# Fourth gated head: both value and gate groups by block products, score levels added on VectorE

## The chip, the core and the metric

The kernel runs on one core of one Trainium2 chip. The metric is the device time of one execution in microseconds (us): 1372.14 us, the median of three runs (1371.32 to 1372.71). One execution was profiled as well; it took 1371.82 us, and its trace spans 1370.1 us from the first to the last instruction.

Five engines work side by side, each through its own queue in order: TensorE (PE in the profile, with its weight loads as PEld), VectorE (DVE), ScalarE (ACT), GpSimd (POOL) and SyncE (SP). The last two issue most of the transfers here. SBUF is the memory that the engines compute from, PSUM holds the sums of the matrix products in banks of 128x512 float32.

## The reference

Two layers over 256 tokens of width 2048: a gated linear attention layer (GLA, 4 heads, chunked), then a retention layer (8 heads). Cut to what matters here, a GLA head computes

```
q, k, v, gate = split(rms_norm(x) @ w_in)
log_a  = log_sigmoid((h @ w_a1) @ w_a2 + b_a) / 16
scores = einsum('bhtk,bhsk,bhtsk->bhts', q * 256**-0.5, k, decay)   # causal, decay from cumsum(log_a)
o      = einsum('bhts,bhsv->bhtv', scores, v) + state part
o      = o * rsqrt(mean(o * o) + 1e-6) * head_g
x      = x + (o * silu(gate)) @ w_out
```

Everything is float32. A head's `v` and `gate` are 1024 columns wide each, which the kernel treats as two groups of 512 columns: head 3 has the groups 6 and 7.

## The kernel before, in words

**Precision.** Each float32 operand of a large product is held as two parts, `hi` and `lo`, of a rounded matrix format, and a product is three matrix products: hi by hi, hi by lo, lo by hi. The activations are split once (`xhl`). The weights come from memory in blocks `raw` of 128x1024 (two slices of 128 rows by 512 columns, called a sub here) and each is split when its turn comes: ScalarE writes `hi` (L298), then VectorE writes `lo` as the difference (L299). There are four buffers for `hi` and four for `lo`, and the code splits up to three subs ahead of the one in use (`LOOK = 3`). A sub that multiplies both halves of the tokens takes twelve 512-column products on TensorE, a sub of a block product (below) takes six.

**A plain group.** `group_x` runs the eight subs of a group for both token halves: 96 products. L341 to L343 are its three products; the results are called `gv_ps` (values) and `gg_ps` (gates).

**A joint pair.** `values_and_gates` computes values and gates of one group together. For the first half of the contraction it replaces the eight block products (two token halves, two halves of the rows, values and gates) by seven, in the manner of Strassen and Winograd; `P1`, `P2`, `P3`, `P5`, `P6`, `P7` and `P8` are these products, 12 matrix products each. The second half is done directly (`v4` to `v7`, `g4` to `g7`, 12 each). The order is the string `UNIT`: `P1 v4 z P3 v5 P5 v6 P6 P2 v7 P7 g4 g5 P8 g6 g7`. The weights' sums are made in place: six transfers per pair, issued by GpSimd, add a block from memory to one already loaded (L310), and two VectorE additions (L293) add one raw block to another. A pair therefore loads 14 blocks plainly and 6 by adding, and splits 22 subs, where two plain groups load and split 16. Its results are called `ge_ps`, its products are L413 to L415. After `P5`, `P6`, `P7`, `v7` and `g7` pieces are copied or combined on ScalarE (L1389, L1394, L1404) and VectorE (L1434, L1437, L1440, L1443, L1395, L1402).

**Which pairs are joint.** `JOINT["a"] = (5, 7)`: groups 5 and 7 of the GLA layer, that is the second groups of heads 2 and 3. Groups 4 and 6 are plain.

**Scores of a head.** `gla_scores` works through seven levels of block size 1 to 64: per level VectorE forms differences of the cumulated decay (L792, L800), ScalarE an exponential (L801), VectorE two products (L802, L803), and TensorE a 128x128 product (L764, `lv`). Then VectorE masks the seven results into `m` (L821, L823), GpSimd adds them level by level into `s32`, two instructions per level (L830), and the sum is split into `sc` (L724, L725). `o_part` multiplies `sc` by the values of a group (L698 to L700). These pieces are generators: `advance()` is called after each sub or block product, and takes one more step of them. For a joint second group, `joint_turn` calls `o_part(0)` after `v4` and `o_part(1)` after `g5`.

**Order and buffers.** The order on each engine is set by the tile framework's scheduler, which places instructions by a simulated timeline; what is written later can thus be placed earlier on its engine, and a piece can be put between other work. Inside an engine nothing overtakes. PSUM banks 0 to 3 (`slots`) rotate: a plain group takes two and rotates by two, a joint pair takes four and rotates by two, and `slots` is set anew to 2, 3, 0, 1 ahead of the output projection `gb`.

Of the kernel before, what the change touches and what calls it, by code (L numbers as in the profile page):

```python
# [15 lines left out]
ALU = mybir.AluOpType  # L16

P = 128
# [143 lines left out]
def ret_order(h):  # L162
# [4 lines left out]
HEAD = 4  # L167
EARLY = 2
JOINT = {
    "a": (5, 7),  # L170
    ("ao", 0): (True, True),
    ("ao", 1): (False, True),
    ("ro", 0): (False, True),
# [5 lines left out]
def kernel(  # L179
# [18 lines left out]
    nc = tc.nc  # L198
# [117 lines left out]
    def advance(n=1):  # L316
        for _ in range(n):
            while side:
                try:
                    next(side[0])  # L320
                    break
                except StopIteration:
                    side.popleft()
# [429 lines left out]
    def gla_scores(h, box):  # L753
# [5 lines left out]
        s32 = sc_p.tile([P, 3, P], F32, tag="s32", name=f"s32_{h}", bufs=1)  # L759
        tt = nc.vector.tensor_tensor  # L760
# [22 lines left out]
        for li, B in enumerate(LEVELS):  # L783
            n = P // B
# [35 lines left out]
        m = t4_p.tile([P, 8, P], F32, tag="t4", name=f"m{h}")  # L820
# [3 lines left out]
        nc.vector.tensor_scalar(s32[:, 1, :], ps[1][:, 3, :], SCALE, None, ALU.mult)  # L824
        yield
        for li, B in enumerate(LEVELS):
            for z in range(2):
                side_of = lambda a, h: a.rearrange("p (n h i) -> p n h i", h=2, i=B)[:, :, h, :]
                dst = side_of(s32[:, 2 * z, :], 1 - z)
                nc.gpsimd.tensor_tensor(dst, dst, side_of(m[:, li, :], z), ALU.add)  # L830
            if li == 3:
                yield
        yield
# [3 lines left out]
    def gla_head(h):  # L837
# [10 lines left out]
        def scores():  # L848
            yield from gla_scores(h, hw)
# [16 lines left out]
        def o_part(gi):  # L866
            g = 2 * h + gi
            if gi == 0:
                drain_side()
            po = [mis_p.tile([P, GW], F32, tag="mis", name=f"go{g}_ps{t}") for t in range(2)]  # L870
            o_mms(hw["sc"], vs[gi], po)
            o = o_p.tile([P, 2, GW], F32, tag="o", name=f"go{g}")
            with tc.high_priority():
                for t in range(2):
                    nc.scalar.activation(o[:, t, :], po[t], AF.Copy, scale=r[:, t : t + 1])
                    nc.scalar.activation(po[t], o[:, t, :], AF.Square, accum_out=sso[:, t, gi : gi + 1])
            os_.append(o)
            if gi == 1:
                side.append(og_part(0))
# [26 lines left out]
            )  # L906

        def joint_turn(tok):
            if tok == "v4":
                o_part(0)  # L910
            elif tok == "g5":
                o_part(1)
            else:
                advance()
# [674 lines left out]
```

## Time and profile before

| What | Value |
| --- | --- |
| time, median of 3 (range) | 1372.14 us (1371.32 to 1372.71) |
| profiled execution | 1371.82 us, span 1370.1 us |
| busy: PE, DVE, ACT, POOL | 1360.1, 1098.9, 846.7, 137.2 us |
| head 3: q and k; group 6 values; group 6 gates; group 7 | from about 448, 472, 497 and 520 us; `gb` begins at 564.8 us |

A row of the timeline reads: start, duration, engine, line and operation, what it writes and reads; in square brackets the idle time before it and what ended that. A row of the groups reads: line, engine, operation, shapes, count, then busy time and mean duration in ns of one, then idle time. In the table by stretches each engine's busy time has its instruction count behind it in brackets, then come the granted TensorE clock, the share of the DMA engines and GB/s. In such rows the line numbers are those of the kernel before.

### The profile page before, as it was taken

To read this page: it belongs to the slowest core of one execution; us is meant where nothing else is said; L and a number is where in the kernel's file an instruction comes from. 1 tells how busy PE (TensorE), PEld (TensorE's weight loads), DVE (VectorE), ACT (ScalarE), POOL (GpSimd) and SP (SyncE) were. 2 spreads that over 40 slices of the span, in tenths; PEclk is the share of its full clock that TensorE was granted. 3 is DMA by queue.
4 is the path that set the end of the run, shared out by engine and by line. 5 is a ranking of instruction groups with operands and counts; after the bars stand their busy time and mean duration, and the time that the engine had idled before them with its cause. 6 is when DMAs were issued, how large, how long until landed. Compare 5 with 4: busy or idle time off the path is not lost.

```text
span 1370.1 us, 18374 instructions
## 1 busy us (share of the span) xinstructions
PE 1360.1 (99%) x6564; PEld 1142.3 (83%) x6564; DVE 1098.9 (80%) x1520; ACT 846.7 (62%) x1119; POOL 137.2 (10%) x194
## 2 busy tenths in 40 slices
PE   9999999999999999999999999999999999999997
PEld 7888888888888888888888888888888888888886
DVE  6686795987878886769887988897867898889796
ACT  6576656656567756656666566655546666666565
POOL 1003020110021021001011010100101101010010
PEclk9999999999999999999999999999999999999999
DMA  9755565789658667868897878796798797879773
GB/s 363 255 175 168 169 208 184 154 251 316 202 154 259 201 207 180 326 169 232 260 336 199 259 203 249 209 320 212 172 365 219 245 253 208 268 188 322 237 177 124
DMA packets 84508, 315.04 MB, mean 230 GB/s; under 512 B 9776, under 2 KB 10800, under 8 KB 83136
## 3 DMA queue, kind: packets, MB, share of 16 engines
q1 hardware_dynamic: 67200, 241.63, 50.6%
q0 software_dynamic: 15920, 64.89, 23.7%
q10 hardware_dynamic: 1296, 7.35, 1.4%
q8 instruction: 51, 0.84, 0.2%
q14 instruction: 41, 0.34, 0.1%
HBM read 303.35 MB, written 10.49 MB: 229 GB/s over the span
## 4 chain that ended last, share of the span: by engine, by line
PE 99%; DMA 1%; DVE 0%; ACT 0%; issue 0%; DVEq 0%; ACTq 0%
PE rqk_ps L382 9%; PE re_ps L413 8%; PE re_ps L414 8%; PE re_ps L415 8%; PE rqk_ps L384 4%; PE gqk_ps L382 4%; PE gg_ps L342 3%; PE gv_ps L343 3%; PE gv_ps L341 3%; PE gv_ps L342 3%; PE gg_ps L343 3%; PE gg_ps L341 3%; PE gqk_ps L384 2%; PE ge_ps L415 2%; PE ge_ps L414 2%; PE ge_ps L413 2%
## 5 line engine op out<-in xcount | busy, mean ns | idle before, releaser
L299 DVE TENSOR_TENSOR lo<-raw,hi 128x1024 fp32r<-128x1024 f32 (+1 forms) x568 | 687.4, 1220 | 215.1 <-ACT hi L298 205.1
L298 ACT ACTIVATE hi<-raw 128x1024 fp32r<-128x1024 f32 (+1 forms) x568 | 596.3, 1056 | 398.9 <-PE rqk_ps L382 50.4
L382 PE MATMUL rqk_ps<-xhl,hi 128*128 128x512 f32 x512 | 160.0, 395 | 0.0
L415 PE MATMUL re_ps<-hi,xhl 128*128 128x512 f32 x352 | 137.1, 389 | 0.0
L414 PE MATMUL re_ps<-lo,xhl 128*128 128x512 f32 x352 | 137.1, 389 | 0.0
L413 PE MATMUL re_ps<-hi,xhl 128*128 128x512 f32 x352 | 132.3, 391 | 0.0
L310 POOL DMA_DIRECT2D raw<-in_w_all x90 | 78.0, 868 | 540.5 <-DVE lo L299 205.2
L384 PEld LDWEIGHTS rqk_ps<-xhl,lo 128*128 128x128 f32 x512 | 93.6, 188 | 20.3
L384 PE MATMUL rqk_ps<-xhl,lo 128*128 128x256 f32 x512 | 99.2, 279 | 0.0
L382 PEld LDWEIGHTS rqk_ps<-xhl,hi 128*128 128x128 f32 x512 | 80.7, 189 | 2.8
L382 PE MATMUL gqk_ps<-xhl,hi 128*128 128x512 f32 x256 | 79.5, 397 | 0.6 <-DVE xhl L550 0.6
L414 PEld LDWEIGHTS re_ps<-lo,xhl 128*128 128x128 f32 x352 | 66.1, 188 | 13.6
L415 PEld LDWEIGHTS re_ps<-hi,xhl 128*128 128x128 f32 x352 | 66.1, 188 | 13.6
L413 PEld LDWEIGHTS re_ps<-hi,xhl 128*128 128x128 f32 x352 | 65.9, 188 | 13.3
L342 PE MATMUL gg_ps<-lo,xhl 128*128 128x512 f32 x192 | 75.4, 393 | 0.0
L343 PE MATMUL gg_ps<-hi,xhl 128*128 128x512 f32 x192 | 75.1, 391 | 0.0
L342 PE MATMUL gv_ps<-lo,xhl 128*128 128x512 f32 x192 | 75.1, 391 | 0.0
L341 PE MATMUL gv_ps<-hi,xhl 128*128 128x512 f32 x192 | 75.0, 393 | 0.0
L341 PE MATMUL gg_ps<-hi,xhl 128*128 128x512 f32 x192 | 74.9, 391 | 0.0
L343 PE MATMUL gv_ps<-hi,xhl 128*128 128x512 f32 x192 | 74.8, 391 | 0.0
L830 POOL TENSOR_TENSOR s<-s,m 128x64 f32<-128x64 f32 x56 | 36.5, 684 | 232.3 <-DVE m L821 222.5
L384 PEld LDWEIGHTS gqk_ps<-xhl,lo 128*128 128x128 f32 x256 | 46.1, 188 | 10.0
(422 smaller groups left out, 2591.9 us busy)
## 6 DMA issues: line engine op xcount, KB each, us to landing
raw<-in_w_all SPq DMA_DIRECT2D x449, 512.0 KB, 4.9
raw<-in_w_all POOLq DMA_DIRECT2D x90, 512.0 KB, 7.2
resid<-in_x_n SPq DMA_DIRECT2D x2, 1024.0 KB, 9.8
gg<-in_gn_g POOLq DMA_DIRECT2D x8, 256.0 KB, 4.4
resid_x<-resid ACTq DMA_DIRECT2D x1, 2048.0 KB, 8.5
gb<-in_gn_b POOLq DMA_DIRECT2D x8, 256.0 KB, 4.9
gb_resid<-resid_x POOLq DMA_DIRECT2D x1, 2048.0 KB, 11.0
resid_g<-gb_resid ACTq DMA_DIRECT2D x1, 2048.0 KB, 9.0
```

The costliest lines, as they stand in the source:

```text
L298: a = nc.scalar.activation(hi[:, sl], src[:, sl], AF.Copy)
L299: b = nc.vector.tensor_tensor(lo[:, sl], src[:, sl], hi[:, sl].bitcast(F32), ALU.subtract)
L310: nc.gpsimd.dma_start(raws[n], block(key), accum_op=ALU.add)
L341: pin(mm(ps, xh, hi[:, q, :], start=kt == 0, stop=False, **onto))
L342: pin(mm(ps, xh, lo[:, q, :], start=False, stop=False, **onto))
L343: pin(mm(ps, xl, hi[:, q, :], start=False, stop=kt == end - 1, **onto))
L382: x = mm(ps[c], part, rhs[:, kt, :, :], start=kt == 0, stop=kt == NKT - 1)
L384: x = mm(ps[c][:, 0, :], part, rhs[:, kt, 0, :], start=False, stop=False)
L413: pin(mm(ps, xh, hi[:, q, :], start=start, stop=False, **again))
L414: pin(mm(ps, xh, lo[:, q, :], start=False, stop=False, **again))
L415: pin(mm(ps, xl, hi[:, q, :], start=False, stop=stop, **again))
L830: nc.gpsimd.tensor_tensor(dst, dst, side_of(m[:, li, :], z), ALU.add)
```

## The change

Group 6, head 3's first, becomes a joint pair like group 7. Since both groups of that head are joint now, `joint_turn` does nothing special in the first of them, and in the second one `o_part(0)` comes after `v6` for head 3 (head 2 keeps `v4`). In all four heads the seven levels are added to `s32` by VectorE instead of GpSimd, with one instruction per level that takes both halves.

```
-    "a": (5, 7),
+    "a": (5, 6, 7),
...
         for li, B in enumerate(LEVELS):
-            for z in range(2):
-                side_of = lambda a, h: a.rearrange("p (n h i) -> p n h i", h=2, i=B)[:, :, h, :]
-                dst = side_of(s32[:, 2 * z, :], 1 - z)
-                nc.gpsimd.tensor_tensor(dst, dst, side_of(m[:, li, :], z), ALU.add)
+            n = P // (2 * B)
+            dst = at(s32, B, (2 * P - B, 2), (2 * B, n), (1, B))
+            tt(dst, dst, at(m, li * P, (B, 2), (2 * B, n), (1, B)), ALU.add)
             if li == 3:
                 yield
...
         def joint_turn(tok):
-            if tok == "v4":
+            if gi and tok == ("v6" if h == 3 else "v4"):
                 o_part(0)
-            elif tok == "g5":
+            elif gi and tok == "g5":
                 o_part(1)
```

One line fewer stands in the new file, so its line numbers after L829 are smaller by one.

How the scheduler places this is seen in three places. The first is VectorE's queue in group 6, between the `lo` of the ninth sub of the group (number 186 of the kernel, both times) and the next; `w3` are the score pieces of head 3, `raw154` and `raw155` the two blocks that are added to. Before:

```order
L299 TENSOR_TENSOR lo186_4395<-raw162_4207,hi186_4394 128x1024
L802 TENSOR_TENSOR w3_5_4410<-w3_5_4410,qk3_4238 128x2x4x32
L803 TENSOR_TENSOR w3_5_4410<-w3_5_4410,qk3_4238 128x2x4x32
L798 TENSOR_TENSOR w3_6_4436<-ref3_4437,lc3_4028 128x2x64
L799 TENSOR_TENSOR w3_6_4436<-lc3_4028 128x2x64
L800 TENSOR_TENSOR w3_6_4436<-lc3_4028 128x2x2x64
L812 TENSOR_TENSOR w3_x_4466<-tot3_4029,lc3_4028 128x256 x2
L299 TENSOR_TENSOR lo187_4421<-raw163_4251,hi187_4420 128x1024
```

Now:

```order
L299 TENSOR_TENSOR lo186_4334<-raw160_4131,hi186_4333 128x1024
L293 TENSOR_TENSOR raw154_3958<-raw154_3958,raw157_4041 128x1024
L802 TENSOR_TENSOR w3_2_4324<-w3_2_4324,qk3_4219 128x2x32x4
L803 TENSOR_TENSOR w3_2_4324<-w3_2_4324,qk3_4219 128x2x32x4
L293 TENSOR_TENSOR raw155_3985<-raw155_3985,raw158_4069 128x1024
L792 TENSOR_TENSOR w3_4_4384<-lc3_4007 128x2x8x16
L800 TENSOR_TENSOR w3_4_4384<-lc3_4007 128x2x8x16
L802 TENSOR_TENSOR w3_3_4351<-w3_3_4351,qk3_4219 128x2x16x8
L803 TENSOR_TENSOR w3_3_4351<-w3_3_4351,qk3_4219 128x2x16x8
L792 TENSOR_TENSOR w3_5_4410<-lc3_4007 128x2x4x32
L800 TENSOR_TENSOR w3_5_4410<-lc3_4007 128x2x4x32
L299 TENSOR_TENSOR lo187_4360<-raw154_3958,hi187_4359 128x1024
```

The two additions of raw blocks now stand between these two splits, and the same sub number meets score work that is two levels further back.

The second place is TensorE's queue around the second to last direct step of group 6 (`g6`, sub 198), in the kernel as changed; `ge6_ps1` and `ge6_ps0` are the gate sums of the two token halves:

```order
L413 MATMUL ge6_ps0_4233<-hi198_4565,xhl_105 128x512
L414 MATMUL ge6_ps1_4234<-lo198_4566,xhl_105 128x512
L415 MATMUL ge6_ps1_4234<-hi198_4565,xhl_105 128x512
L413 MATMUL ge6_ps1_4234<-hi198_4565,xhl_105 128x512
L414 MATMUL ge6_ps1_4234<-lo198_4566,xhl_105 128x512
L415 MATMUL ge6_ps1_4234<-hi198_4565,xhl_105 128x512
```

Products that need only `hi198` are put ahead of the first that needs `lo198`, which VectorE writes.

The third is GpSimd's queue through head 3. Before, the last of the level additions, one load and the transfers of group 7:

```order
L830 TENSOR_TENSOR s_3_4272<-s_3_4272,m_4502 128x4x16 x2
L1244 DMA gg_6778<-in_gn_g 128x512
L830 TENSOR_TENSOR s_3_4272<-s_3_4272,m_4502 128x2x32 x2
L830 TENSOR_TENSOR s_3_4272<-s_3_4272,m_4502 128x64 x2
L310 DMA raw_4447<-in_w_all 128x1024
L310 DMA raw_4481<-in_w_all 128x1024
```

Now, the six transfers of group 6, the same load, and the first of group 7:

```order
L310 DMA raw_3958<-in_w_all 128x1024
L310 DMA raw_3985<-in_w_all 128x1024
L310 DMA raw_4041<-in_w_all 128x1024
L310 DMA raw_4069<-in_w_all 128x1024
L310 DMA raw_3958<-in_w_all 128x1024
L310 DMA raw_3985<-in_w_all 128x1024
L1243 DMA gg_6776<-in_gn_g 128x512
L310 DMA raw_4459<-in_w_all 128x1024
```

All additions of levels are gone from it; it holds only transfers here.

## The prediction

> **What bounds the kernel now.** I read the page first, then TensorE's waits over the whole span, then head 3 by stretches.
>
> ```profile
> span 1370.1 us, 18374 instructions
> PE 1360.1 (99%) x6564; PEld 1142.3 (83%) x6564; DVE 1098.9 (80%) x1520; ACT 846.7 (62%) x1119; POOL 137.2 (10%) x194
> PE 99%; DMA 1%; DVE 0%; ACT 0%; issue 0%; DVEq 0%; ACTq 0%
> L830 POOL TENSOR_TENSOR s<-s,m 128x64 f32<-128x64 f32 x56 | 36.5, 684 | 232.3 <-DVE m L821 222.5
> ...
> PE warm_ps L522 <- POOL lnone L524: 1.0, 1, 1.0
> PE gqk_ps L382 <- DVE xhl L550: 0.6, 1, 0.6
> PE zps L641 <- DVE wa L615: 0.5, 1, 0.5
> ```
>
> The chain that ends last is 99% TensorE, and TensorE's complete list of waits is 2.1 us, all at the start. So a matrix product less is time saved, in full, as long as nobody else becomes late. GpSimd's 36.5 us of level additions are hidden: taking them away gains nothing by itself.
>
> ```profile
> 472.00:497.20 25.20, 25.20 (x127) 21.31 (x126) 24.09 (x49) 16.29 (x23) 2.38 (x4) 1.00 0.55 185
> 497.20:520.00 22.80, 22.80 (x106) 19.00 (x106) 17.14 (x21) 11.34 (x13) 7.94 (x14) 1.00 0.73 199
> 520.00:565.00 45.00, 45.00 (x200) 37.27 (x199) 34.20 (x40) 31.60 (x43) 3.98 (x5) 1.00 0.85 272
> ```
>
> These are group 6's values, its gates, and the joint pair of group 7 (columns: length, PE, PEld, DVE, ACT, POOL, clock, DMA). VectorE is busy 24.09 of 25.2 us in the first: that is head 3's score work beside the splits. TensorE does not wait there because the next stretch, 17.14 of 22.8, lets VectorE run behind and catch up inside its lead of three subs. Over the three, VectorE has 93.0 - 75.4 = 17.6 us free.
>
> **What the change removes.** Group 6 falls from 192 products of 512 columns to 84 + 96 = 180.
>
> ```profile
> 402.21 0.39 PE L341 MATMUL gg_ps<-hi,xhl 128*128 128x512 f32 x1
> ...
> 404.48 0.39 PE L414 MATMUL ge_ps<-lo,xhl 128*128 128x512 f32 x1
> ```
>
> Ten products start between these rows: 2.27 us, 0.227 us each (the 0.39 us are one product's passage, not its share of time). Twelve fewer: **-2.7 us**. The Trainium skill (TensorE: Matmul & The Clock Gate, Part 1, "Wait — 56ns, not 53.3ns?") gives a warm product N divided by 2.4 GHz plus 2.5 ns, 215.7 ns for 512 columns. By that the saving would be 2.6 us, and, as TensorE would reach each sub of group 6 earlier, the lateness worked out below would be 158 times 0.011 us, 1.8 us, larger, for a time near 1375.5. The row differs from the page, and the row decides.
>
> **What it adds on VectorE.** Prices, from the groups of 472 to 565 us:
>
> ```profile
> L299 DVE TENSOR_TENSOR lo<-raw,hi 128x1024 fp32r<-128x1024 f32 x38 | 46.2, 1222 | 14.5 <-ACT hi L298 14.0
> L293 DVE TENSOR_TENSOR raw<-raw,raw 128x1024 f32<-128x1024 f32 x2 | 2.4, 1223 | 0.0
> L1395 DVE SCALAR_TENSOR_TENSOR gv<-ge,rr,gv 128x512 fp32r<-128x512 f32 x2 | 1.5, 748 | 0.8 <-ACT gv L1394 0.8
> L812 DVE TENSOR_TENSOR w_x<-tot,lc 128x256 f32<-128x256 f32 x2 | 0.8, 418 | 0.0
> L1440 DVE TENSOR_TENSOR ge<-ge_ps,ge 128x512 f32<-128x512 f32 x1 | 0.7, 685 | 0.0
> L814 DVE TENSOR_TENSOR w_x<-w_x,qk 128x256 f32<-128x256 f32 x1 | 0.6, 569 | 0.0
> L823 DVE TENSOR_TENSOR m<-lv,mask 128x384 f32<-128x384 f32 x1 | 0.5, 545 | 0.0
> L799 DVE TENSOR_TENSOR w<-lc 128x128 f32<-128x128 f32 x1 | 0.3, 284 | 0.0
> ```
>
> But what the queue pays is the step from start to start:
>
> ```profile
> 473.53 1.22 DVE L299 TENSOR_TENSOR lo<-raw,hi 128x1024 fp32r<-128x1024 f32 x1
> ...
> 482.42 1.22 DVE L299 TENSOR_TENSOR lo<-raw,hi 128x1024 fp32r<-128x1024 f32 x1
> 483.56 0.42 DVE L807 TENSOR_TENSOR s<-dg,mask 128x256 f32<-128x256 f32 x1
> 483.89 0.42 DVE L802 TENSOR_TENSOR w<-w,qk 128x256 f32<-128x256 f32 x1
> 484.22 0.42 DVE L803 TENSOR_TENSOR w<-w,qk 128x256 f32<-128x256 f32 x1
> ```
>
> A split of 1.22 us holds it 1.14, an operation of 0.42 us holds it 0.335: 0.083 less than its duration. The pair adds six splits and two raw additions (8 x 1.14 = 9.1), five 512-wide combinations (5 x 0.60 = 3.0; its two L1395 take the place of two evacuations), and the seven level additions. Those are not in the trace; 128 elements cost 0.284 in L799, so 0.2 held each, 1.4 a head (bounds: 0.2 by that row, 0.335 by the 256-wide rows). Sum 13.5 us, in a stretch that is 2.7 us shorter: of 17.6 us free, 1.4 stay. VectorE would be about 98% held, so what counts is where in the stretch the work lies. In heads 0 to 2 the 1.4 us fall beside plain groups, where the second row above has 5.7 us free in 22.8; nothing there, and 1.4 us each if that cover were gone.
>
> **Where it lies.** From the `lo` of sub 181 on, which starts at 473.53 before and has the same queue ahead of it now, to that of sub 198 (step `g6`), the new VectorE queue holds 67 instructions: 18 splits (20.5), two raw additions and two of 1024 elements for the output sums (4.6), 32 of 256 (10.7), six of 512 (3.6), two L502 (0.8) and five smaller ones (1.7): 41.9, and the last one's own end, 42.0. I take the uncontended 0.42 for L814, whose 0.57 fell beside GpSimd's additions. Sub 198 is ready at 515.5.
>
> ```profile
> 472.06 0.48 PE L341 MATMUL gv_ps<-hi,xhl 128*128 128x512 f32 x1
> ...
> 498.60 0.60 PE L764 MATMUL lv<-w 128*128 128x128 f32 x4
> ```
>
> TensorE begins the group at 472.1. Ahead of its first product with `lo198` stand 158 products (35.9 us), 16 score products in two passes (four passes take 0.60 us with the last one's passage, so 0.1 each, 3.2 us) and 4 small ones (0.4): wanted at 511.6. **Late by 3.9 us.** The same count gives 1.4 us at sub 187, after the raw additions, and 2.3 us at 191; after 198 it falls to 2 us by sub 203, since the score work is done. TensorE loses the largest lateness once, in pieces: **+4.0 us**. Bounds: below, no loss if score work slid behind the splits (the queue is fixed, so that is far); above, 67 x 0.083 = 5.6 us more if nothing overlapped.
>
> ScalarE must not be the later one: 22 `hi`, 7 exponentials and the pair's copies, as in the third stretch with 31.60 of 45 us busy, plus 7 x 0.63 for the exponentials. That makes 36 of 43, so it fits.
>
> The six added transfers go through GpSimd's queue:
>
> ```profile
> raw<-in_w_all SPq DMA_DIRECT2D x449, 512.0 KB, 4.9
> raw<-in_w_all POOLq DMA_DIRECT2D x90, 512.0 KB, 7.2
> ```
>
> The tightest are the two that follow the raw additions: by the count above the second addition ends at 489.2, 0.9 for the issue and 7.2 to the landing make 497.3, and the `hi` that needs them stands before sub 193's `lo`, at 502.0. 3 us of room, used up only by a landing of 10 us or more. The load of `gg` ahead of group 7's transfers waits for the last reader of the mask (L823, at 511.2 by the count); those transfers are due after the splits of subs 200 and 201, at 518.7 and 520. SyncE's queue has two loads fewer and nothing new ahead of it.
>
> **A bank.** Group 6 as a pair rotates the banks by two instead of four, so `gb`'s first sum now uses a bank that group 7's gates have just held; before, its banks had been free since the values.
>
> ```profile
> 564.57 0.39 PE L415 MATMUL ge_ps<-hi,xhl 128*128 128x512 f32 x1
> 564.59 0.68 DVE L1402 TENSOR_TENSOR gsg<-ge_ps,gsg 128x512 f32<-128x512 f32 x1
> 564.80 0.39 PE L341 MATMUL gb_ps<-hi,ogt 128*128 128x512 f32 x1
> ```
>
> L1402, which empties it, ended at 565.27, and `gb` began at 564.80: **+0.5 us** (0 to 1.2, a `lo` ahead of it).
>
> `o_part(0)` after `v6` puts six products where `sc` should be done: by the two counts, carried on, VectorE finishes `sc` (L725) at 529.7, and TensorE asks for it at 527.5 plus the 4.0 it lost. 1.8 us of room: nothing, and past that each us late costs one. After `v4`, four products earlier, it would have waited.
>
> **The sum.** 1371.82 - 2.7 + 4.0 + 0.5 = 1373.6 for the profiled execution, which is 0.3 below the median: **1373.9 us**, 0.13% slower. I take 0.2% (2.74 us, so 1369.4 and 1374.9) as what a measurement can tell from no change.
>
> **Rivals.**
> 1. *ScalarE holds VectorE up*: slower. Each L802 waits for its exponential, which now stands behind denser `hi` splits. For it: VectorE's queue has no slack to absorb a wait. Against: in the stretches above VectorE waits for ScalarE only at splits. A `hi` of 1.06 us that starts just ahead costs its remainder, between nothing and 7 x 1.06 us over the seven levels; with 0.3 us each the loss is 2.1 us more: 1376.0. It decides from 1.0 us on, where 1374.9 is passed.
> 2. *The splits keep up*: the added work goes where VectorE idled (14.0 us waiting for `hi`), and TensorE's products with `hi` alone, placed ahead, cover the rest. Against: 3.9 us are more than the five or six products placed ahead (0.227 each). Time 1371.82 - 2.7 + 0.5 + 0.3 = 1369.9, or 1369.4 without the bank.
> 3. *Later scores*: `sc` misses `v6`, so moving `o_part` doesn't do what it should; with VectorE 4 us later there than counted, 2.2 of them beyond the room, 1376.1.
>
> **Chances.** Forecast 0.58 (its own range 1372.6 to 1375.4, of which 0.07 lies over 1374.9), rival 1 0.22, rival 2 0.14 (half of it under 1369.4), rival 3 0.06. So faster by over 0.2% has 0.07, slower 0.07 + 0.22 + 0.06 = 0.35, within 0.58. The range 1370.0 to 1376.3 leaves out half of rival 2 and the upper end of rival 1; nothing overlapping, 1379.5, is too far to be held.
>
> **What would show it.** Right: 6552 PE instructions with a total that stays 12 x 0.227 lower outside the waits; TensorE waits of about 4 us in all for `lo` L299 between 490 and 516 us, none over 1.5 us; VectorE without idle time from 474 to 515; one wait of about 0.5 us for L1402 where `gb` begins; no L830 on POOL. Wrong: no waits for `lo` (rival 2); VectorE waiting for L801 (rival 1); TensorE waiting at L698 (rival 3); or waits outside head 3, where I expect none.

## The result, and the profile after

| | Before | After |
| --- | --- | --- |
| time, median (range) | 1372.14 us (1371.32 to 1374.25, 9 runs) | 1374.95 us (1374.69 to 1377.51, 9 runs) |
| ratio, 95% interval | | 1.0023 (1.0012 to 1.0033) |
| profiled execution, span | 1371.82 us, 1370.1 us | 1374.95 us, 1373.2 us |
| products of TensorE | 6564 | 6552 |

The changed kernel is 2.8 us slower: the middle of the interval lies just beyond the 0.2% drawn as the bound, the interval itself on both sides of it. The prediction was 1373.9 us, with 1370.0 to 1376.3 as the range.

From the page of the changed kernel, its span, its first line of busy times and its chain of waits (in its rows, lines from L830 on carry a number one lower than before, so L1388 is the old L1389):

```profile
span 1373.2 us, 18353 instructions
PE 1359.9 (99%) x6552; PEld 1141.0 (83%) x6552; DVE 1114.6 (81%) x1561; ACT 852.7 (62%) x1129; POOL 105.7 (8%) x144
PE 89%; DMA 4%; DVE 3%; issue 2%; ACT 1%; POOL 0%; DVEq 0%; ACTq 0%; POOLq 0%
```

Twelve products are gone, but the chain that ends last was 99% TensorE and is 89% now: transfers and VectorE have come into it. TensorE's waits over the whole span of the changed kernel (total, times, longest; the waits of the start of the program and one of 0.2 us at 327 us are left out):

```profile
PE ge_ps L413 <- ACT gsg L1388: 1.3, 1, 1.3
...
PE go_ps L698 <- ACT gv L1393: 0.8, 1, 0.8
PE ge_ps L414 <- DVE lo L299: 0.7, 2, 0.5
PE gb_ps L341 <- DVE hm L887: 0.5, 1, 0.5
```

A wait in this list begins when the product ahead has left the array, so it is a little shorter than what TensorE loses. The loss itself is read from the starts of consecutive products, less their usual distance of 0.227 us:

| Place in the changed kernel | Lost | What TensorE waits for |
| --- | --- | --- |
| 491 to 500 us, group 6, subs 187 and 188 | 1.75 us | `lo` (L299); 0.3 us of it for a `hi` |
| 507.0 us, group 6, first product after `P7` | 1.6 us | the copy L1388 of `P7` |
| 551.0 us, `o_part(1)` of head 3 | 1.1 us | the split of the values, L1393 |
| 567.2 us, first product of `gb` | 0.7 us | the bank of the gates |
| 639.6 us, the pair of `gb` | 0.4 us | a bank that VectorE empties (L1000) |

That is 5.55 us; with 0.1 more than before elsewhere, and 2.7 less for the twelve products, the last product starts 2.97 us later than before (1364.93 against 1361.96). So the loss is explained to a tenth of a microsecond; the question is what makes these five places.

Three stretches of the changed kernel (length, PE, PEld, DVE, ACT, POOL, clock, share of the DMA engines, GB/s):

```profile
472.00:490.00 18.00, 18.00 (x88) 15.09 (x87) 17.97 (x34) 13.68 (x19) 1.35 (x2) 1.00 0.40 106
490.00:516.00 26.00, 23.85 (x113) 19.12 (x112) 26.00 (x41) 16.45 (x21) 2.63 (x4) 1.00 1.02 296
516.00:562.00 46.00, 45.17 (x199) 37.07 (x198) 38.98 (x46) 32.76 (x43) 5.74 (x7) 1.00 0.87 259
```

VectorE is busy without a gap for 44 us, as counted. What was not counted stands in the last but one column: from 490 to 516 us the DMA engines are taken entirely, where before they were at 0.55 and 0.73 in that region. ScalarE around the wait at 507 us, and again at 551 us:

```profile
498.94 1.05 ACT L298 ACTIVATE hi<-raw 128x1024 fp32r<-128x1024 f32 x1
504.45 2.00 ACT L298 ACTIVATE hi<-raw 128x1024 fp32r<-128x1024 f32 x2 [4.46 <-DMA raw<-in_w_all]
506.36 0.58 ACT L1388 ACTIVATE gsg<-ge_ps 128x512 f32<-128x512 f32 x1
...
549.23 1.06 ACT L298 ACTIVATE hi<-raw 128x1024 fp32r<-128x1024 f32 x1 [3.02 <-DMA raw<-in_w_all]
550.20 0.71 ACT L1393 ACTIVATE gv<-ge,rr 128x512 fp32r<-128x512 f32 x1
```

Both times ScalarE stands still for a weight block that has not landed, and what TensorE needs (L1388, L1393) is queued behind that `hi`. VectorE and TensorE at the first of the two:

```profile
505.26 1.24 DVE L299 TENSOR_TENSOR lo<-raw,hi 128x1024 fp32r<-128x1024 f32 x1
```

```profile
505.05 0.60 PE L764 MATMUL lv<-w_x 128*128 128x128 f32 x4
506.99 0.50 PE L413 MATMUL ge_ps<-hi,xhl 128*128 128x512 f32 x1 [1.33 <-ACT gsg L1388]
507.33 0.40 PE L414 MATMUL ge_ps<-lo,xhl 128*128 128x512 f32 x1
```

The `lo` in the VectorE row is that of sub 194, which the third TensorE row uses. It ended at 506.50 and could not have been used sooner. So two things are late by nearly the same amount here, and the profile names only the later one: the copy, ready at 506.94, and VectorE's split, ready at 506.50. Only experiments tell them apart.

### The profile page after: what moved, and what is told of

Same layout as the page of the kernel before. It is cut to its first block, busy times and chain, and to the rows that moved or that the text cites. A ratio compares the mean times of both kernels' runs of the same rounds, so it can differ in the third digit from the quotient of the medians.

```text
span 1373.2 us, 18353 instructions
## 1 busy us (share of the span) xinstructions
PE 1359.9 (99%) x6552; PEld 1141.0 (83%) x6552; DVE 1114.6 (81%) x1561; ACT 852.7 (62%) x1129; POOL 105.7 (8%) x144
## 4 chain that ended last, share of the span: by engine, by line
PE 89%; DMA 4%; DVE 3%; issue 2%; ACT 1%; POOL 0%; DVEq 0%; ACTq 0%; POOLq 0%
PE rqk_ps L382 9%; PE re_ps L413 8%; PE re_ps L414 8%; PE re_ps L415 8%; PE rqk_ps L384 4%; PE gqk_ps L382 4%; DMA raw<-in_w_all 3%; PE gg_ps L342 3%; PE gv_ps L343 3%; PE gg_ps L343 3%; PE gv_ps L341 3%; PE gg_ps L341 3%; PE gv_ps L342 3%; PE ge_ps L413 2%; PE ge_ps L415 2%; PE ge_ps L414 2%
## 5 line engine op out<-in xcount | busy, mean ns | idle before, releaser
L299 DVE TENSOR_TENSOR lo<-raw,hi 128x1024 fp32r<-128x1024 f32 (+1 forms) x574 | 694.9, 1220 | 208.4 <-ACT hi L298 197.0
L310 POOL DMA_DIRECT2D raw<-in_w_all x96 | 83.0, 869 | 706.2 <-DVE lo L299 369.6
L342 PE MATMUL gg_ps<-lo,xhl 128*128 128x512 f32 x160 | 63.0, 394 | 0.0
L343 PE MATMUL gg_ps<-hi,xhl 128*128 128x512 f32 x160 | 62.7, 392 | 0.0
L342 PE MATMUL gv_ps<-lo,xhl 128*128 128x512 f32 x160 | 62.5, 391 | 0.0
L341 PE MATMUL gg_ps<-hi,xhl 128*128 128x512 f32 x160 | 62.4, 391 | 0.0
L341 PE MATMUL gv_ps<-hi,xhl 128*128 128x512 f32 x160 | 62.3, 393 | 0.0
L343 PE MATMUL gv_ps<-hi,xhl 128*128 128x512 f32 x160 | 62.3, 390 | 0.0
L414 PE MATMUL ge_ps<-lo,xhl 128*128 128x512 f32 x132 | 51.5, 390 | 0.0
```

Source lines behind the costliest of these rows:

```text
L299: b = nc.vector.tensor_tensor(lo[:, sl], src[:, sl], hi[:, sl].bitcast(F32), ALU.subtract)
L310: nc.gpsimd.dma_start(raws[n], block(key), accum_op=ALU.add)
L341: pin(mm(ps, xh, hi[:, q, :], start=kt == 0, stop=False, **onto))
L342: pin(mm(ps, xh, lo[:, q, :], start=False, stop=False, **onto))
L343: pin(mm(ps, xl, hi[:, q, :], start=False, stop=kt == end - 1, **onto))
L414: pin(mm(ps, xh, lo[:, q, :], start=False, stop=False, **again))
```

## The experiments

Two theories. **Theory 1**: VectorE's queue in group 6 is too full, so its splits are late. **Theory 2**: the weight transfers are late, and ScalarE's queue, in order, hands that on. Beside them stands the question which of the three parts of the change costs what. All ratios are to the kernel before, run on the same chip in the same session.

| Run | Group 6 | Level additions | `o_part(0)` | Other edit | Ratio (95% interval) |
| --- | --- | --- | --- | --- | --- |
| the change | pair | VectorE | `v6` | | 1.0023 (1.0012 to 1.0033) |
| e1_levels | plain | VectorE | `v6` | | 1.0015 (1.0007 to 1.0024) |
| e5_lev_v4 | plain | VectorE | `v4` | | 1.0002 (0.9993 to 1.0011) |
| e10_pair_v4 | pair | VectorE | `v4` | | 1.0017 (1.0008 to 1.0026) |
| e6_pair_pool | pair | GpSimd | `v6` | | 1.0030 (1.0019 to 1.0041) |
| e12_pair_only | pair | GpSimd | `v4` | | 1.0027 (1.0016 to 1.0038) |
| e2_sums | pair | VectorE | `v6` | sums for `gb` later | 1.0005 (0.9997 to 1.0014) |
| e3_noacc | pair | VectorE | `v6` | four added transfers left out | 1.0024 (1.0015 to 1.0034) |
| e4_bank | pair | VectorE | `v6` | banks of `gb` | 1.0032 (1.0019 to 1.0045) |
| e7_spread | pair | VectorE | `v6` | score work spread | 1.0011 (1.0002 to 1.0019) |
| e8_all | pair | VectorE | `v4` | e2, e7 and banks together | 1.0000 (0.9991 to 1.0009) |
| e11_all_noacc | pair | VectorE | `v4` | e8, four added transfers left out | 0.9987 (0.9978 to 0.9996) |
| e9_order | pair | VectorE | `v4` | e8, `P8` ahead of `g5` | 0.9996 (0.9988 to 1.0005) |

### e1_levels and e5_lev_v4: the parts without the pair

```
-    "a": (5, 6, 7),
+    "a": (5, 7),
```

> Group 6 computed plainly again (192 products); the level additions on VectorE and the later o_part(0) of head 3 stay. First theory (all of the loss comes from the pair of group 6): 1371.8 for the profiled run and 1372.1 for the median, ratio 1.000 within 0.0004; TensorE has no wait of 0.3 us or more between 470 and 640 us. Rival (the additions themselves cost, 7 x 0.2 us held in head 3, where VectorE had 1.1 us free in 472 to 497): up to 1.4 us more, 1373.5, with waits for lo L299 in head 3.

Measured: 1373.96 us against 1371.67. Neither theory held: there is no wait in head 3, and yet 1.3 us are lost, in `gb`. TensorE's waits in that kernel, without those of the start:

```profile
PE gb_ps L341 <- ACT ogt L501: 0.6, 1, 0.6
```

`gb` multiplies `ogt`, the normed and gated output of head 3, and it is not there in time. That points to the third part of the change, so it was undone next:

```
-            if gi and tok == ("v6" if h == 3 else "v4"):
+            if gi and tok == "v4":
```

> Group 6 plainly, the level additions on VectorE as in e1_levels, but o_part(0) of head 3 back at v4. Theory (what e1_levels lost, 1.4 us of waits for ogt in gb, comes from o_part(0) at v6: the output sums of head 3, and with them its norm, stand later in the queues): no wait for ogt at 577 us, the norm (hm) begins near 561.5 us as before, time equal to the kernel before, ratio 1.000. Rival (the additions on VectorE push the norm back): the waits for ogt stay, ratio 1.0015.

Measured: 1371.94 us against 1372.18, and no wait of TensorE after the start. The norm of head 3 on VectorE, first row with `o_part(0)` at `v6` (e1_levels), second at `v4` (e5_lev_v4):

```profile
564.80 0.15 DVE L887 TENSOR_TENSOR hm<-sso 128x2 f32<-128x2 f32 x1
```

```profile
561.09 0.16 DVE L887 TENSOR_TENSOR hm<-sso 128x2 f32<-128x2 f32 x1
```

So the level additions on VectorE cost nothing that can be measured, and `o_part(0)` at `v6` costs 1.3 us when group 6 is plain. It is not `o_part(0)` itself that costs: its first product starts at 522.20 us in e1_levels and at 522.19 in e5_lev_v4. The planner put the pieces of `o_part(1)` later: its last product starts at 560.96 in e1_levels and at 558.69 in e5_lev_v4, and what follows (the norm above, then scaling, transposes and `ogt`) is up to 4 us later. Why the planner moved `o_part(1)` along was not tried.

### e10_pair_v4, e6_pair_pool, e12_pair_only: the parts with the pair

e10_pair_v4 has the last diff above on top of the change; e6_pair_pool has this one, and e12_pair_only both.

```
-            tt(dst, dst, at(m, li * P, (B, 2), (2 * B, n), (1, B)), ALU.add)
+            nc.gpsimd.tensor_tensor(dst, dst, at(m, li * P, (B, 2), (2 * B, n), (1, B)), ALU.add)
```

> The changed kernel with o_part(0) of head 3 back at v4; pair and level additions on VectorE stay. Theory A (o_part(0) at v6 costs in gb, as e1_levels against e5_lev_v4 showed, 1.4 us): 1373.6, ratio 1.0013, and the norm of head 3 (hm) 3 us sooner. Theory B (with the pair, sc is ready only after v6 anyway, and what v6 costs in gb lies beside the bank's wait): 1374.9, ratio 1.0023. Theory C (my forecast's reason for v6: TensorE would ask for sc 4 products too early): a wait of 1 to 2 us at L698 near 528 us, ratio 1.003.

Measured: 1373.88 us against 1371.87. Theory C is out: with `o_part(0)` at `v4` TensorE does not wait for `sc`. But it does not ask sooner either: the planner starts `o_part(0)` at 531.82 us here and at 531.60 in the changed kernel, after `sc` is ready (529.85 and 529.63). So `v4` against `v6` is not a test of what an earlier `o_part(0)` would wait for. Between A (1.0013) and B (1.0023) the measured 1.0017 does not decide. In the profiled execution 0.2 us are left of the 1.1 lost near 551 us, the 0.4 at the pair of `gb` are gone, and the loss at the bank of `gb` is 1.0 instead of 0.7 us; that execution took 1374.95 us, 1.1 above its median. At 551 us the split L1393 is no sooner than in the changed kernel (551.01 against 550.20); `o_part(1)` begins six products later in TensorE's queue, 62 products ahead of the first of `gb` instead of 68.

> The changed kernel with the level additions on GpSimd again, one operation for both halves of a level; pair and o_part(0) at v6 stay. Theory 1 (VectorE's queue in group 6 is what costs; the additions come after the wait at 505 us, so they are no part of it): the waits at 490 to 507 us stay at 3.3 us, ratio 1.0023 as the changed kernel. Rival (the seven additions, 1.4 us held, are part of the loss): the wait at 549 us (1.1) goes, ratio 1.0013; against it, GpSimd's queue would issue the accumulating transfers of group 7 later, which would give it back.

Measured: 1375.80 us against 1372.18, a ratio above both expectations, though its interval overlaps that of the change. e12_pair_only was to complete the four cases:

> The pair of group 6 alone: level additions on GpSimd (one operation for both halves of a level), o_part(0) of head 3 at v4. With e10_pair_v4 (1.0017: additions on VectorE) and e6_pair_pool (1.0030: o_part(0) at v6) it completes the four cases of the pair. Theory (parts add up: o_part(0) at v6 costs about 0.06% with the pair, as from e10 to the changed kernel, and GpSimd's additions cost about 0.07% against VectorE's): 1.0024. Rival (with the pair, GpSimd's slow additions make sc late at v4, where TensorE asks for it earlier): 1.003 or more, with a wait at L698 of over 1 us.

Measured: 1376.03 us against 1371.97, between both expectations. Its waits of TensorE between 510 and 530 us, and its level additions on GpSimd between 505 and 540 us:

```profile
PE ge_ps L414 <- DVE lo L299: 1.1, 1, 1.1
PE go_ps L698 <- ACT sc L724: 1.0, 1, 1.0
```

```profile
L829 POOL TENSOR_TENSOR s<-s,m 128x128 f32<-128x128 f32 x7 | 7.5, 1070 | 0.5
```

The same line on VectorE in the changed kernel, in the same stretch:

```profile
L829 DVE TENSOR_TENSOR s<-s,m 128x128 f32<-128x128 f32 x7 | 2.1, 305 | 0.0
...
L454 DVE TENSOR_TENSOR osum_f<-osum_y,osum_y 128x512 f32<-128x512 f32 x1 | 0.7, 717 | 0.0
```

Seven additions take 7.5 us on GpSimd and 2.1 on VectorE, and while GpSimd adds, `sc` is late and so is a `lo`. These two waits (2.5 us lost with their neighbours) are in both GpSimd variants and in neither of the VectorE ones. So with the pair, moving the additions to VectorE is worth about 0.1% (1.0027 to 1.0017, 1.0030 to 1.0023; each pair of intervals overlaps, the waits in the profiles are what shows it). The pair by itself costs 0.27% (e12_pair_only), and with the additions on VectorE 0.15% (1.0017 in e10_pair_v4 against 1.0002 in e5_lev_v4). Whether `v6` adds to that is not shown by these ratios.

### e2_sums: work taken out of VectorE's queue

The planner puts the sums of `ogt` that the joint pair of `gb` needs from 607 us on as early as 504 us, since their inputs are there. Here their additions are kept in program order, which puts them behind group 7's value splits:

```
+        tt = (lambda *x: keep(nc.vector.tensor_tensor(*x))) if name == "late" else nc.vector.tensor_tensor
...
-                side.append(make_sums(ogt, "osum", sums_in_v))
+                side.append(make_sums(ogt, "late", sums_in_v))
```

> The changed kernel, with the sums of ogt for the later joint pair of gb (L449 to L458) kept behind the value splits of group 7, so that two operations of 1.13 us held and four of 0.6 leave VectorE's queue between 504 and 530 us. Theory 1 (VectorE's queue is too full): the lo of sub 194 ends 1.1 us sooner, and of the 1.5 us wait at 505 us about 1.1 goes; time 1373.8. The waits for lo at 490 to 499 us (1.7 us) stay, since nothing ahead of them changes. Theory 2 (the weight transfers are late, and ScalarE's queue holds the copy L1388 behind the hi splits that wait for them): the waits at 505 us (1.5) and at 549 us (1.0) stay as they are, 1374.9.

Measured: 1373.06 us (1371.25 to 1373.98) against 1371.67. TensorE's waits between 480 and 660 us, and below them ScalarE's wait for weights between 484 and 512 us:

```profile
PE ge_ps L414 <- DVE lo L299: 0.7, 2, 0.5
PE gb_ps L341 <- DVE hr_nw L496: 0.5, 1, 0.5
```

```profile
ACT hi L298 <- DMA raw<-in_w_all: 4.6, 1, 4.6
```

The loss at 507 us falls from 1.6 to 0.5 us, those at 551 and 639 us are gone, and the 1.75 at the subs 187 and 188 stay: Theory 1 at 507 us, although ScalarE waits for its block as long as in the changed kernel. How a shorter VectorE queue makes a late copy harmless is read from the order on TensorE. After `P7` come the products of sub 194 on two banks: `ps1` (B), which is free, and `ps0` (A), which the copy L1388 must empty. In the changed kernel, then in e2_sums:

```
L764 MATMUL lv3_1_4259<-w3_x_4480 128x128 x2
L413 MATMUL ge6_ps0_4233<-hi194_4488,xhl_105 128x512
L414 MATMUL ge6_ps1_4234<-lo194_4489,xhl_105 128x512
...
L764 MATMUL lv3_1_4259<-w3_x_4480 128x128 x2
L414 MATMUL ge6_ps1_4234<-lo194_4489,xhl_105 128x512
L415 MATMUL ge6_ps1_4234<-hi194_4488,xhl_105 128x512
```

In the changed kernel the planner placed the product that needs only `hi` first, on the bank that waits for the copy, and the whole queue stands behind it; with the sums out of the way it begins with six products on the free bank, 1.4 us that cover most of the wait for the copy. That its timeline did so because `lo194` is late there is argued, not shown. The loss at 551 us does not go because the split of the values is sooner (L1393 at 550.73, against 550.20): `o_part(1)` begins 57 products ahead of the first of `gb` here, 68 in the changed kernel. In the profiled execution of e2_sums another 1.8 us are lost between 316 and 330 us (0.4 in the changed kernel), before anything that the edit touches; it was the slowest of its runs, and its last product starts 2.0 us after that of the kernel before.

### e3_noacc: transfers taken away

```
-        for n, key in post:
+        for n, key in post if i not in (187, 188) else ():
```

> The changed kernel without the four accumulating transfers that follow the raw additions of group 6 (the products P7 and P8 then use sums without a part of the weights, so the output is not the reference's). Theory 2 (transfers): the four hold all 16 engines from 488 to 502 us and keep the plain load for sub 195, issued at 495.5, from landing before 504.4; without them it lands about 4 us after its issue, ScalarE's idle 4.5 us goes, and with it the waits of TensorE at 505 us (1.5 us) and, as the loads behind it come sooner too, part of the 1.0 at 549 us: 1373.0 to 1373.5. Theory 1 (VectorE): the lo of sub 194 still ends at 506.5, and TensorE, which needs it by 505.4, still waits 1.1 us there: 1374.5 to 1374.9. By both the 1.7 us at 490 to 499 us stay.

Measured: 1374.69 us against 1371.67, the same ratio as the change. TensorE's waits between 480 and 660 us:

```profile
PE ge_ps L414 <- DVE lo L299: 0.9, 3, 0.5
PE go_ps L698 <- ACT gv L1393: 0.6, 1, 0.6
PE gb_ps L341 <- DVE hm L887: 0.5, 1, 0.5
PE ge_ps L413 <- ACT gsg L1388: 0.2, 1, 0.2
```

ScalarE now waits for no block between 484 and 512 us, so the burst of added transfers was what kept it. The load of sub 195 is issued at 495.42 us here and lands 4.2 us later; in the changed kernel it is issued at 495.50 and takes 8.8. So it was not issued too late, it landed too late. But TensorE gains next to nothing: the copy costs 0.4, then `lo194` costs 0.5, and 0.5 more come at 515 us, for the `lo` of sub 198. Up to there it loses 3.2 us without the added transfers and 3.4 with them. **Theory 2 alone falls**: behind the late transfer stands VectorE with nearly the same lateness.

### e4_bank: the bank of `gb`

```
     get_resid("gb_resid")
-    slots = deque((2, 3, 0, 1))
+    slots = deque((0, 1, 2, 3))
```

> The changed kernel with the banks of gb begun two further on, so that its first sum uses a bank which group 7's values left, not the one its gates have just held. Theory (the wait of 0.7 us at 566 us is the bank alone): that wait goes, 1374.3. Rival (the first products of gb are held by the next thing in line, the splits of gb's first subs behind L1402 or the norm of head 3): the time stays at 1374.9, with a wait of the same size under another name between 565 and 580 us.

Measured: 1375.81 us against 1371.67. The wait for the bank is gone, and this one is there, at 578 us, 1.3 us with its neighbours:

```profile
PE gb_ps L341 <- ACT ogt L501: 0.6, 1, 0.6
```

It is the wait of e1_levels: 48 products of `gb`, then eight transposes of head 3's output in a row, then the wait for `ogt`. In the changed kernel the planner begins `gb` on one of its two banks and puts products between and behind those transposes, so that there is other work while the norm of head 3 is finished. The 0.7 us at the bank go and 1.3 us at `ogt` come; that the order of the banks is the whole reason is argued. The interval overlaps that of the change, so the times do not show that this version is slower.

### e7_spread and e8_all: score work out of group 6

```
-            else:
+            elif gi or h < 3 or tok not in ('v4', 'P3', 'P5', 'g4'):
                 advance()
```

> The changed kernel with head 3's score work spread out: at four of the fifteen turns of group 6 (v4, P3, P5, g4) nothing of it is put into the queues, so that it runs on into group 7. The transfers and the operations are the same. Theory 1 (the score work of 474 to 500 us fills VectorE's queue ahead of the splits): about four operations of 0.335 us, 1.3 us, leave the queue ahead of the lo of sub 187; the waits at 490 to 499 us go from 1.7 to about 0.5 us, the one at 505 us (1.5) goes, and the time is 1372.3 to 1373.0. Rival (what is put off comes back as a wait for sc at o_part(0), or the transfers are late all the same): as much is lost at L698 near 530 us, 1374.5 to 1375.

Measured: 1373.35 us against 1372.18. TensorE's waits between 480 and 660 us:

```profile
PE ge_ps L413 <- ACT gsg L1388: 0.9, 1, 0.9
PE ge_ps L413 <- ACT hi L298: 0.5, 1, 0.5
PE ge_ps L414 <- DVE lo L299: 0.4, 1, 0.4
```

The loss for `lo` at 490 to 500 us falls from 1.75 to 0.6 us and nothing comes back at L698 (0.7 us do at 538 us, for a `lo`): Theory 1 holds for that place. But the loss at 507 us does not go, it is 2.0 us now, for a `hi` and for the copy L1388. With VectorE less full, the transfers are what is left there; e11_all_noacc tests that.

e8_all puts e7_spread, e2_sums, `v4` and other banks (`1, 2, 3, 0`) together.

> The changed kernel with four edits: the sums for gb kept behind group 7's value splits (as e2_sums), head 3's score work spread (as e7_spread), o_part(0) at v4, and the banks of gb begun one back. Theory 1: of the 6.3 us of waits about 1 us is left, at 490 us, and the twelve products saved (2.7) show: 1.5 to 2.0 us faster than the kernel before, ratio 0.9987. Rival (the waits are handed on to ogt in gb, as in e4_bank): 1.3 us of wait at 577 us, ratio 0.9997.

Measured: 1372.20 us against 1372.18. Of the five places two are left, 0.5 us at 490 us and 1.3 at 506 us. TensorE's only wait between 480 and 660 us, and ScalarE's for weights between 484 and 512 us:

```profile
PE ge_ps L413 <- ACT gsg L1388: 0.9, 1, 0.9
```

```profile
ACT hi L298 <- DMA raw<-in_w_all: 5.0, 1, 5.0
```

In this profiled execution 1.4 us more are lost at 914 to 917 us, for a `lo` of the retention layer, where the kernel before lost nothing.

### e11_all_noacc and e9_order: the transfers, with VectorE out of the way

e11_all_noacc is e8_all with the diff of e3_noacc.

> e8_all without the four accumulating transfers that follow group 6's raw additions (P7 and P8 use sums without a part of the weights, so the output is not the reference's). Theory (the burst of four, 488 to 502 us, is what keeps the load of sub 195 waiting): the 5.0 us for which ScalarE waits for a load before 503 us go, and with them the wait of 1.3 us at 505 us; ratio to before 0.9991. Rival (SyncE's queue sends that load too late by itself, its buffer being free only after the lo of sub 189): the wait shrinks by less than half.

Measured: 1370.35 us against 1371.87. The list of TensorE's waits is empty between 480 and 660 us (by the starts, 0.6 us are still lost at 490 us, 0.5 in e8_all), and ScalarE waits for no block between 484 and 512 us. So **Theory 2 holds too, behind Theory 1**: the same removal that was worth nothing in the changed kernel takes away the 1.3 us at 506 us, 0.1% of the time, once VectorE keeps up. The ratios say 0.13% (1.0000 and 0.9987), with intervals that just touch.

e9_order gets at the same wait with all the work done. In groups 6 and 7 `P8`, whose blocks should have landed by then, goes ahead of `g5`, whose load is late:

```
-P1 v4 z P3 v5 P5 v6 P6 P2 v7 P7 g4 g5 P8 g6 g7
+P1 v4 z P3 v5 P5 v6 P6 P2 v7 P7 g4 P8 g5 g6 g7
```

> e8_all with one edit more: in groups 6 and 7 the product P8 stands between the gates' subs g4 and g5, not behind both, in the order of the subs and of the loads. In e8_all one wait of 1.3 us is left at 505 us: the copy L1388, which empties the bank that the gates go on with, stands in ScalarE's queue behind the hi of g5, and that waits for its load (a plain one, issued at about 495 us, landing at 503.0 behind the accumulating transfers). Theory 2 in this narrow form (late transfer, then the queue): P8's weights have landed by 501, so the copy comes right after P7 and the wait goes: 1.2 us faster than e8_all, 1371.0, ratio to before 0.9991. Rival (VectorE's splits are as late as the copy): nothing changes, 1372.2, ratio 1.0000.

Measured: 1371.17 us (1370.27 to 1373.43) against 1371.87. ScalarE in it:

```profile
499.12 1.06 ACT L298 ACTIVATE hi<-raw 128x1024 fp32r<-128x1024 f32 x1 [1.02 <-PE ge_ps L415]
502.85 1.06 ACT L298 ACTIVATE hi<-raw 128x1024 fp32r<-128x1024 f32 x1 [2.67 <-DMA raw<-in_w_all]
503.82 0.58 ACT L1388 ACTIVATE gsg<-ge_ps 128x512 f32<-128x512 f32 x1
```

The copy comes 1.1 us sooner than in e8_all (504.94), 0.4 us of it because TensorE is that much earlier here, and the loss falls from 1.3 to 0.9 us, not to nothing: the second block of `P8` lands at 502.8, later than expected. The profiled execution took 1370.40 us, 1.4 less than that of the kernel before, and its last product starts at 1360.37. But the interval of the ratio, 0.9988 to 1.0005, holds 1: that this version beats the kernel before is likely and not shown.

## Why the prediction was right or wrong

**The saving, -2.7 us: right.** TensorE has 6552 products, and outside the five places they stand 0.227 us apart as before. The alternative with 215.7 ns from the Trainium skill (TensorE: Matmul & The Clock Gate, Part 1, "Wait — 56ns, not 53.3ns?") came to 1375.5 us. That is nearer to the result, but by luck: the distance did not change and the splits were not later than counted.

**VectorE's count: right.** The `lo` of sub 198 was to end at 515.5 us; it ended at 515.3. The stretch without idle time was to last from 474 to 515 us and does. An addition of a level was to take 0.284 us; it takes 0.305 here, and none of the seven costs anything (e5_lev_v4).

**+4.0 us for TensorE's waits for `lo`: the right mechanism, 0.6 us too large, and half of it under another name.** Up to sub 198 TensorE lost 3.4 us: 1.75 at the first subs, nearly all for `lo`, and 1.6 at 507 us, where the copy L1388 was the last to come. That the largest lateness is lost once, in pieces, held: without the late transfer 3.2 us are lost up to the same `lo` (e3_noacc), so VectorE alone accounts for nearly the whole sum. The first piece goes with less score work ahead of it (e7_spread), most of the second with the sums moved (e2_sums). At 507 us a late transfer lies beside VectorE, nearly as late. The prediction had one cause for this sum; at that place there are two, and taking away one leaves the other. Rival 2, by which the splits keep up, fell: there are waits for `lo`.

**"3 us of room" for the transfers: the question was too narrow.** The count asked whether the added blocks land in time, and they do: the `hi` of sub 192 follows at 496.53 without a wait. It did not ask what they do to the plain loads. The load for sub 195, issued at 495.50, found the DMA engines taken by the added ones, and ScalarE waited for it from 500.0 to 504.45 us. In this kernel that costs little, 0.2 us (3.4 against the 3.2 of e3_noacc); with VectorE out of the way it is 1.3 us (e8_all against e11_all_noacc).

**ScalarE "fits": wrong in kind.** By work it fits: 16.45 of 26 us busy. But it stood still 4.46 us in its queue with the copy behind it. Rival 1 had ScalarE as the late engine, at the exponentials and through VectorE; that did not happen, VectorE never waits for L801 in this stretch.

**The bank, +0.5 us: right in place and size (0.7), but not to be had back.** With other banks 1.3 us are lost at `ogt` instead (e4_bank), since the norm of head 3 is late for `gb`. It is late with `o_part(0)` at `v6`: it begins at 564.80 us in e1_levels and at 561.09 in e5_lev_v4, at 566.98 in the changed kernel and at 563.61 in e10_pair_v4.

**`o_part(0)` after `v6` at no cost: the count was right, the price wrong.** `sc` was to be ready at 529.7 and asked for at 531.5 us; it was ready at 529.63 and asked for at 531.60. So rival 3, a late `sc`, did not happen. The cost lies in what the planner does with the pieces behind it, `o_part(1)` above all: 1.3 us in the kernel with group 6 plain. In the changed kernel the ratios put it at 0.06% (1.0023 against 1.0017, with intervals that overlap), so its size there stays open.

**Waits that the sum put at nothing: 1.5 us, the largest miss.** `o_part(1)`, still in head 3, lost 1.1 us at L698, and the pair of `gb`, outside it, 0.4, where the prediction expected none. At 551 us TensorE waits for the split L1393, which stands behind a late block in ScalarE's queue. Such a block was there before the change too, without a wait of TensorE:

```profile
547.53 1.06 ACT L298 ACTIVATE hi<-raw 128x1024 fp32r<-128x1024 f32 x1 [2.32 <-DMA raw<-in_w_all]
548.50 0.71 ACT L1394 ACTIVATE gv<-ge,rr 128x512 fp32r<-128x512 f32 x1
```

The split is 1.7 us later now, and `o_part(1)` begins 68 products ahead of the first of `gb`, where it was 62. In e2_sums and e10_pair_v4 the split is no sooner than in the changed kernel, but `o_part(1)` begins 57 and 62 products ahead, and at most 0.2 us are lost; in e3_noacc and e4_bank, where it is 68 again, 0.9 and 1.3 us are. So what decides here is where the planner puts `o_part(1)`; why it put it there was not tried. The 0.4 us at 639.6 us stay open: L1000, which empties the bank, stands behind a `lo` whose `hi` had waited 1.52 us for its block, and the loss is gone in e2_sums, e3_noacc and e10_pair_v4 alike.

In numbers: 4.5 us of waits were forecast, 5.7 came (3.4 + 0.7 + 1.5 + 0.1). The difference of 1.2 is, but for rounding, the 1.1 us between 1373.9 and 1374.95, and it carried the result over the bound of 0.2%. That it is no more is partly luck: the 0.6 us too much for `lo` hid part of the 1.5 that were put at nothing.

## What to carry to other kernels

When an engine's queue is full, ask what the transfers do in that same stretch: here VectorE and the DMA engines were late by nearly the same amount at the same place, and taking away either one alone showed only part of the gain or none of it (e3_noacc 1.0024, e11_all_noacc 0.9987). Count what added transfers take from the plain loads that run beside them, and whatever is queued behind a load's consumer, not only when they land themselves. Before removing a small wait, look at what becomes ready during it: without the 0.7 us at the bank, 1.3 us were lost at `ogt`. And where a planner sets the order, look in the trace for what an edit moved: `v6` instead of `v4` left the start of `o_part(0)` where it was and moved `o_part(1)`.

## What the runs showed of the hardware

**A transfer that adds holds the DMA engines twice as long.** Two stretches of the changed kernel, the first with adding transfers alone, the second with plain loads but for a few packets:

```profile
491.00:498.00 7.00, 6.19 (x25) 4.49 (x25) 7.00 (x13) 5.70 (x9) 1.71 (x2) 1.00 1.05 201
503.00:512.00 9.00, 7.67 (x36) 6.27 (x35) 9.00 (x13) 5.11 (x6) 0.57 (x1) 1.00 1.02 401
```

Both times all engines are busy, at 201 GB/s when they add and at 401 when they load. The queues (packets, MB, share of the 16 engines; q0 are GpSimd's transfers, q1 SyncE's), from 491 to 498 us with the landing of the plain loads issued in that stretch, and from 498 to 501 us:

```profile
q0 software_dynamic: 390, 1.40, 105.3%
q1 hardware_dynamic: 1, 0.00, 0.2%
...
raw<-in_w_all SPq DMA_DIRECT2D x3, 512.0 KB, 9.3
```

```profile
q0 software_dynamic: 89, 0.36, 67.3%
q1 hardware_dynamic: 91, 0.37, 34.7%
```

From 498 to 501 us the two move the same number of bytes, and the adding ones take twice the engines' time for it. A plain load of 512 KB that is issued among them took 9.3 us to land (median of three), against 3.7 in the kernel before between 470 and 525 us. The Trainium skill (DMA: Bandwidth & Descriptors, "Issuing engines are not separate DMA queues") says that transfers run on the same 16 engines and interleave, whichever engine issues them. The trace agrees from 498 us on. Ahead of that it does not show it: the three plain loads were issued at 495.50, 495.92 and 496.97 us, and SyncE's queue moved one packet up to 498.

**A strided addition of 128 elements takes 1070 ns on GpSimd and 305 on VectorE**, and VectorE's own work beside it is stretched: L454, 717 ns in the changed kernel, takes 1008 ns in e12_pair_only, where it lies among GpSimd's additions:

```profile
L454 DVE TENSOR_TENSOR osum_f<-osum_y,osum_y 128x512 f32<-128x512 f32 x1 | 1.0, 1008 | 0.0
```

The Trainium skill (SBUF — State Buffer, "SBUF: two separate sides") has VectorE and GpSimd share a pair of ports that one instruction holds for its whole length, when VectorE reads two operands from SBUF and GpSimd reads SBUF too. The row agrees with that: L454 reads two, and is longer by less than one GpSimd addition. L1442, which takes one operand from PSUM and lies among the same additions, is not stretched: 715 ns in the changed kernel, 677 here:

```profile
L1442 DVE TENSOR_TENSOR ge<-ge_ps,ge 128x512 f32<-128x512 f32 x1 | 0.7, 677 | 0.0
```
